# Seven products of halves for two pairs of down blocks in each half of the feed-forward layers

## The chip, the core and the metric

The kernel runs on one core of a Trainium2 chip. A core has a matrix engine (TensorE, PE in the profile, with its weight loads shown apart as PEld), a vector engine (VectorE, DVE), an activation engine (ScalarE, ACT), a general engine (GpSimd, POOL) and a queue engine (SyncE, SP). Each works through its own instructions strictly in the order of the program and waits on semaphores that other engines and transfers raise. The metric is device time in microseconds (us), the median of several runs.

## The reference

One decoder layer on 256 prompt tokens and 8 single-token samples, 264 tokens in all, model width 2048:

```python
def swiglu(x, wg, wu, wd):
    return (jax.nn.silu(x @ wg) * (x @ wu)) @ wd
...
h = h + 0.5 * swiglu(rmsnorm(h, norm_ffn1[l]), ffn1_gate[l], ffn1_up[l], ffn1_down[l])
mix, C_f, n_f, m_f, buf = mixing_block(rmsnorm(h, norm_mix[l]), w_in[l], ...)
h = h + mix
h = h + 0.5 * swiglu(rmsnorm(h, norm_ffn2[l]), ffn2_gate[l], ffn2_up[l], ffn2_down[l])
y = rmsnorm(h, norm_final)
```

The feed-forward width is 5504, or 43 blocks of 128. All inputs are float32. The change touches the down products (`@ wd`) of both feed-forward layers.

## The kernel before

Everything lies transposed: features on the 128 partitions, the 264 tokens in the free dimension. `h` is the running state in 16 blocks of 128 features; two neighbours share a tile (`hpair`). A float32 product is made of float16 parts: every operand is cut into a high part `hi` (ScalarE, `high`, L220) and a low part `lo` = rest (VectorE, `low`, L228), and each 128x128 weight block is three matmuls over 264 columns (`three`, L287 to L289): hi by x hi, hi by x lo, lo by x hi.

**Order of the program.** Layer 1, then the mixing block, then layer 2, then the final norm. A layer is worked in two halves of its 43 blocks: blocks 0 to 21, then 22 to 42. In each half first all gate and up products of its blocks (16 weight blocks each, "gate-up stage"), which leave the activations `a` of 22 or 21 blocks, then 16 down products over these ("down stage"), each added to one block of `h` (L846, VectorE). In the second half `done(db)` follows each of them: in layer 1 it cuts the block for the mixing block and squares it on GpSimd, in layer 2 it squares it and scales it with the final gain on ScalarE. The last two down products of layer 2 are made in two spans of tokens by `end`.

**Weights.** `plan` lists pieces of at most 8 weight blocks in the order of use. `fetch` issues a piece's transfer on SP, its hi on ScalarE and its lo on VectorE. `product` calls `fetch` after each piece that it consumes, so that five pieces (AHEAD) are under way or ready; hi, lo and raw have six buffers each. In a gate-up stage `lag` holds a piece's lo back until the next fetch, so that it stands behind the next piece's hi; in a down stage it was off. `tick` counts products (and halves of them); `at(delta, fn)` puts work into the program at a later tick, so the order on every engine is what this hand-made agenda gives.

**Seven products.** For 23 blocks (SEVEN) gate and up are not two plain products. Their 2 x 16 weight blocks are taken as a 2 x 2 matrix of halves, the tokens as two halves of 132, and seven products of halves (Strassen's scheme in Winograd's form) give the four quarters: 7 x 8 x 3 = 168 matmuls over 132 columns (L409) where two plain products have 2 x 16 x 3 = 96 over 264. `chunk_by_seven` issues them in two parts, c = 0 (72 matmuls, weights `sa`) and c = 1 (96 matmuls, weights `sb`), with one plain block between them. `by_seven` puts the quarters together on VectorE (tile `y7`, L759 to L763). The activations' sums of halves, `forms`, are made once by `form` (ScalarE and GpSimd, L659 to L665) and `form_split`.

**Preparing their weights.** `prepare` makes a list of steps for each such job, and `prepare_step` performs one step after each piece that `product` consumes, up to `step_end`: load raw weights through GpSimd's queue (`load`, L331, two buffers), hi and lo of the plain quarters (`blocks`, `blocks_low`, tile `sa`), the sums of quarters (`all_sums`, L355 to L357, tile `ssum`; hi and lo of them in `sb`). A job has eight steps, and in a gate-up stage one job is needed every three blocks, which have eight pieces. At the end of the first half `step_end` stops the steps, and four more are allowed at the start of its down stage.

Two checks run beside the work: `watch` sums a strip of each product (L537), and `judge_early` (L556 to L580) compares all sums so far with bounds; it stands at the start of the product of block 7 in layer 2's last down stage.

## Time and profile before

| | us |
|---|---|
| time, median of 3 runs | 1816.19 (1815.84 to 1818.47) |
| the profiled execution, its own time | 1816.65 |
| its span in the trace | 1814.9 |
| layer 1: down stage of the first half | 242.80 to 361.98 |
| layer 1: gate-up of the second half | 361.98 to 580.80 |
| layer 1: down stage of the second half | 580.80 to 694.29 |
| layer 2: the same three stages | 1348.68 to 1467.87, to 1686.69, to 1794.54 |

The stage borders are the starts of TensorE's first matmul of each stage in the timeline. TensorE is busy for 1797.8 us, VectorE for 1388.2, ScalarE for 953.1 and GpSimd for 237.2. The granted TensorE clock is 0.998 of full speed over the run. A matmul's busy time in the profile has a modelled end, so what one costs is read from the distance between two starts, not from its duration. Idle time behind a row stands in brackets with what ended it.

### The profile page before, as it was taken

How to read it: one execution, taken by the hardware profiler on the slowest of the kernel's cores; microseconds unless marked ns; L12 is line 12 of the kernel's file. 1: busy time of each engine (PE TensorE's matmuls, PEld its weight loads, DVE VectorE, ACT ScalarE, POOL GpSimd, SP SyncE). 2: the span in 40 equal slices, each digit the busy share in tenths (PEclk: the TensorE clock that was granted, in tenths of full speed). 3: DMA queues.
4: the chain of work that ended last, by engine and by line, in shares of the span. 5: the costliest groups of instructions: out<-in, count | busy, mean ns of one | idle time of the engine just before them, and what ended most of it. 6: DMA issues, size and time to landing. Idle time of an engine off the chain costs nothing. (4 is left out here: it accounts for less than half of the span.)

```text
span 1814.9 us, 42526 instructions
## 1 busy us (share of the span) xinstructions
PE 1797.8 (99%) x17918; PEld 1591.0 (88%) x17918; DVE 1388.2 (76%) x2141; ACT 953.1 (53%) x1329; POOL 237.2 (13%) x338
## 2 busy tenths in 40 slices
PE   9999999999999999999999999999999999999997
PEld 7889988899998888888888888899988889999886
DVE  7888975579997657788888766789986459998564
ACT  7664554445554444567566645655554335554442
POOL 0310000000100222222121022410000001010110
PEclk9999999999999999999999999999999999999999
DMA  8665666645654565888887655756567646564553
GB/s 301 243 222 168 219 208 230 203 153 189 215 192 153 185 193 189 302 284 276 280 283 238 222 180 185 254 191 220 191 193 249 199 148 215 191 207 153 191 186 101
DMA packets 118615, 381.34 MB, mean 210 GB/s; under 512 B 15084, under 2 KB 24908, under 8 KB 118416
## 3 DMA queue, kind: packets, MB, share of 16 engines
q1 hardware_dynamic: 95952, 302.29, 50.1%
q0 software_dynamic: 21504, 75.81, 12.2%
q8 instruction: 142, 2.33, 0.5%
q10 hardware_dynamic: 960, 0.45, 0.1%
q14 instruction: 57, 0.47, 0.1%
HBM read 366.72 MB, written 11.78 MB: 209 GB/s over the span
## 5 line engine op out<-in xcount | busy, mean ns | idle before, releaser
L228 DVE SCALAR_TENSOR_TENSOR wlo<-wraw,whi 128x1024 f16<-128x1024 f32 (+2 forms) x600 | 688.2, 1172 | 103.5 <-ACT whi L220 102.9
L220 ACT ACTIVATE whi<-wraw 128x1024 f16<-128x1024 f32 (+2 forms) x600 | 580.0, 1000 | 160.6 <-PE ps L288 140.7
L289 PE MATMUL ps<-x,wlo 128*128 128x264 f16 x1952 | 538.8, 276 | 1.1 <-DVE wlo L228 1.1
L287 PE MATMUL ps<-x,whi 128*128 128x264 f16 x1952 | 538.8, 276 | 0.2 <-ACT whi L220 0.2
L288 PE MATMUL ps<-x,whi 128*128 128x264 f16 x1952 | 538.8, 276 | 0.0
L289 PEld LDWEIGHTS <-wlo 128*128 128x128 f16 x4522 | 442.5, 98 | 67.4 <-DVE wlo L228 2.4
L288 PEld LDWEIGHTS <-whi 128*128 128x128 f16 x4522 | 442.4, 98 | 66.2
L287 PEld LDWEIGHTS <-whi 128*128 128x128 f16 x4522 | 442.7, 98 | 65.6 <-issue 0.6
L289 PE MATMUL ps<-a,wlo 128*128 128x264 f16 (+2 forms) x1418 | 382.7, 273 | 0.4 <-DVE wlo L228 0.4
L287 PE MATMUL ps<-a,whi 128*128 128x264 f16 (+2 forms) x1418 | 382.8, 273 | 0.0
L288 PE MATMUL ps<-a,whi 128*128 128x264 f16 (+2 forms) x1418 | 382.8, 273 | 0.0
L287 PE MATMUL ps<-xm,whi 128*128 128x264 f16 x896 | 247.3, 276 | 0.0
L289 PE MATMUL ps<-xm,wlo 128*128 128x264 f16 x896 | 247.3, 276 | 0.0
L288 PE MATMUL ps<-xm,whi 128*128 128x264 f16 x896 | 247.3, 276 | 0.0
L220 ACT ACTIVATE sb<-ssum 128x2048 f16<-128x2048 f32 x46 | 87.9, 1911 | 181.2 <-DVE ssum L357 181.2
L409 PEld LDWEIGHTS <-sb 128*128 128x128 f16 x2208 | 128.8, 98 | 0.7
L846 DVE SCALAR_TENSOR_TENSOR h<-ps,h 128x264 f32<-128x264 f32 x62 | 26.7, 431 | 126.7 <-PE ps L289 126.7
L228 DVE SCALAR_TENSOR_TENSOR sb<-ssum,sb 128x2048 f16<-128x2048 f32 x46 | 105.2, 2288 | 8.0 <-ACT sb L220 5.6
L409 PE MATMUL ps<-f,sb 128*128 128x132 f16 x1656 | 99.0, 221 | 0.0
L409 PEld LDWEIGHTS <-sa 128*128 128x128 f16 x1656 | 97.1, 98 | 0.7
L331 POOL DMA_DIRECT2D sraw<-in_w2gu x48 | 34.6, 723 | 420.7 <-issue 371.5
L228 DVE SCALAR_TENSOR_TENSOR sa<-sraw,sa 128x1536 f16<-128x1536 f32 x46 | 81.8, 1778 | 3.1
(255 smaller groups left out, 1601.7 us busy)
## 6 DMA issues: line engine op xcount, KB each, us to landing
wraw<-in_w2gu SPq DMA_DIRECT2D x124, 512.0 KB, 4.6
wraw<-in_w1gu SPq DMA_DIRECT2D x120, 512.0 KB, 4.8
wraw<-in_win SPq DMA_DIRECT2D x112, 512.0 KB, 5.7
wraw<-in_w1d SPq DMA_DIRECT2D x80, 448.0 KB, 4.0
wraw<-in_w2d SPq DMA_DIRECT2D x80, 448.0 KB, 4.1
sraw<-in_w2gu POOLq DMA_DIRECT2D x48, 512.0 KB, 4.9
sraw<-in_w1gu POOLq DMA_DIRECT2D x44, 512.0 KB, 5.3
wraw<-in_wout SPq DMA_DIRECT2D x32, 512.0 KB, 4.8
```

Source lines behind the costliest of these rows:

```text
L220: nc.scalar.activation(dst, src, AF.Copy, scale=scale)
L228: nc.vector.scalar_tensor_tensor(dst, src, scale, hi, op0=ALU.mult, op1=ALU.subtract)
L287: nc.tensor.matmul(ps, wh, xk[:, 0, :], start=first, stop=False)
L288: nc.tensor.matmul(ps, wh, xk[:, 1, :], start=False, stop=False)
L289: nc.tensor.matmul(ps, wl, xk[:, 0, :], start=False, stop=last)
L331: queue.dma_start(raw[:, 2 * g : 2 * g + 2], blocks[:, :, ks[c], :])
L409: nc.tensor.matmul(out, w[:, f, k, :], b(k)[:, part, :], start=(k + term == 0), stop=(k == 7 and term == 2),)
L846: nc.vector.scalar_tensor_tensor(h[db], ps, 0.5 / (sw * sa[layer]), h[db], op0=ALU.mult, op1=ALU.add)
```

## The change

Two pairs of down blocks in each half of each layer, blocks (6, 7) and (10, 11), now go by seven products over the first 16 of the half's activation blocks; the remaining 6 (first half) or 5 (second half) blocks of each are a short plain product ("rest"). A pair's parts alternate with plain blocks: part 0, block 8, rest 6, part 1, block 9, rest 7, and likewise for 10 and 11 with 12 and 13. The raw weights of these pairs come through GpSimd's queue, as jobs of the same list of steps. For the right-hand side `form` adds hi and lo of two activation blocks on GpSimd, makes their sums there, and `form_split` cuts them (ScalarE, VectorE): eight forms for each half, started with the up product of the half's last block. The steps pause from that block's start until down block 3, and afterwards no job is prepared before the one before it has been begun. The sums of weights are written over the raw weights instead of into `ssum`, and the loads into these buffers stand after the low part of the sums. In the down stages `lag` is on. Also: `Norm.cut` gives the low part of a block one tick later, `judge_early` stands at the last product before `end`, two kinds of checking tiles use `y7`'s buffer, and some tiles of the mixing block have buffers in other pools.

```diff
+SEVEN_DOWN = {"1": ((3, 5), (3, 5)), "2": ((3, 5), (3, 5))}
 PAIRS = sum(len(v) for v in SEVEN.values())
+PAIRS += sum(len(v) for halves in SEVEN_DOWN.values() for v in halves)
...
+def down_order(pairs, n):
+
+    order = []
+    for p in range(-(-n // 2)):
+        if p in pairs:
+            for c in range(2):
+                order += [("seven", p, c), ("one", 2 * p + 2 + c), ("rest", 2 * p + c)]
+        elif p - 1 not in pairs:
+            order += [("one", db) for db in range(2 * p, min(2 * p + 2, n))]
+    return order
...
+        jobs = []
+        for half, blocks_ in enumerate(HALVES):
+            jobs += [(j, gu[j, 0], gu[j, 1]) for j in SEVEN[layer] if j in blocks_]
+            cut = slice(blocks_[0], blocks_[0] + KB)
+            for p in SEVEN_DOWN[layer][half]:
+                jobs.append((("d", half, p), d[2 * p][:, cut], d[2 * p + 1][:, cut]))
...
-            sums[0] = s = pool.tile([128, 4, 4, 128], F32, tag="ssum", name="ssum")
-            nc.vector.tensor_tensor(s[:, 2], raw[:, 2], raw[:, 3], op=ALU.add)
-            nc.vector.tensor_tensor(s[:, 3], s[:, 2], raw[:, 1], op=ALU.subtract)
+            nc.vector.tensor_tensor(raw[:, 3], raw[:, 2], raw[:, 3], op=ALU.add)
+            nc.vector.tensor_tensor(raw[:, 1], raw[:, 3], raw[:, 1], op=ALU.subtract)
...
-                s = -4 if n == 0 else 8 * n + (-2, -1)[c]
+                s = -4 if n == 0 else 8 * n + (-2, 0)[c]
                 steps.setdefault(s, []).append((load, j, c))
...
         hi, lo = formed.pop((j, c))
+        step_end[0] += 8 * (c == 0)
...
+            def form(k):
+                b = form_blocks()
+                for n, i in enumerate((k + 8, k)):
+                    y = act[blocks[i]]
+                    side.tensor_tensor(
+                        b[:, 2 * n : 2 * n + 2].rearrange("p s t -> p (s t)"), y[:, 0, :],
+                        y[:, 1, :], op=ALU.add,
+                    )
+                forms.append(form_sums(b))
...
-                    if half_size and half == 0 and j == blocks[-1]:
-
-                        step_end[0] = step_no[0]
                     lag[0] = half_size and j >= (3 if start is not None else 1)
+                    if downs and j == blocks[-1]:
+
+
+                        paused, step_end[0] = step_end[0], min(step_end[0], step_no[0] + 1)
+                        for k in range(9):
+                            when = 2 + int(1.5 * k) / 2
+                            if k:
+                                at(when, form_split, k - 1)
+                            if k < 8:
+                                at(when, form, k)
...
-                if half == 0 and half_size:
-                    step_end[0] += 4
+                lag[0] = bool(downs)
...
+                def down_by_seven(p):
+                    y, halves = assemble(seven.pop(p))
+
+                    def summed():
+                        both = hpair[p].rearrange("p i t -> p (i t)")
+                        nc.vector.scalar_tensor_tensor(
+                            both, y[:, 0:4].rearrange("p s t -> p (s t)"), scale, both,
+                            op0=ALU.mult, op1=ALU.add,
+                        )
+
+                    at(1, halves)
+                    at(1, summed)
+
+                for kind, db, *c in down_order(downs, KB - apart):
+                    if kind == "seven":
+                        if c[0] == 0:
+                            seven[db] = [bank() for _ in range(3)]
+                        chunk_by_seven(("d", half, db), c[0], x, forms, seven[db])
+                        if c[0] == 1:
+                            down_by_seven(db)
+                        continue
+                    if downs and db == 3:
+                        step_end[0] = paused
+                    over = range(KB if kind == "rest" else 0, len(x))
+                    ps = product((layer, "d", half, db), x, over)
...
                 lag[0] = False
                 release()
-                for db in range(KB - apart):
...
-        at(2 * NFB + 2 * KB - 8, judge_early)
+
+        more = 2 * sum(len(p) for p in SEVEN_DOWN["2"])
+        at(2 * NFB + 2 * KB + more - 2, judge_early)
```

Three places show how instructions move. Names: `wlo` is the lo of a plain piece (896 is 7 weight blocks, 1024 is 8, 768 is 6), `sraw` the raw weights of a seven-job, `sb` the lo of its sums, `fa` the lo of a form, `h` an update of the state, `stat` a watched strip, `y` and `twins` the putting together.

VectorE, first half's down stage, near its end. Before, from the update of block 12 on, each product had an update, its strip and three lo parts:

```order
L846 SCALAR_TENSOR_TENSOR h_86<-ps,h_86 128x264
L537 TENSOR_REDUCE stat<-ps 128x1
L228 SCALAR_TENSOR_TENSOR wlo<-wraw,whi 128x896
L228 SCALAR_TENSOR_TENSOR wlo<-wraw,whi 128x1024
L228 SCALAR_TENSOR_TENSOR wlo<-wraw,whi 128x896
L846 SCALAR_TENSOR_TENSOR h_86<-ps,h_86 128x264
```

And now, from the state's update by the second pair (blocks 10 and 11) to the update of block 13:

```order
L919 SCALAR_TENSOR_TENSOR h_85<-y_5049,h_85 128x528
L248 SCALAR_TENSOR_TENSOR wlo<-wraw,whi 128x896
L381 TENSOR_TENSOR sraw<-sraw 128x512
L382 TENSOR_TENSOR sraw<-sraw 128x512
L383 TENSOR_TENSOR sraw<-sraw 128x2x512
L248 SCALAR_TENSOR_TENSOR wlo<-wraw,whi 128x896
L248 SCALAR_TENSOR_TENSOR sb_5085<-sraw,sb_5084 128x4x512
L248 SCALAR_TENSOR_TENSOR wlo<-wraw,whi 128x1024
L381 TENSOR_TENSOR sraw<-sraw 128x512
L382 TENSOR_TENSOR sraw<-sraw 128x512
L383 TENSOR_TENSOR sraw<-sraw 128x2x512
L939 SCALAR_TENSOR_TENSOR h_86<-ps,h_86 128x264
```

Behind these stand the strip, one more `wlo` of 896, the second `sb`, the update of block 11 with its strip, and the `wlo` of block 15's second piece. The sums of a job stand now inside the down stage, ahead of the lo parts that TensorE needs next.

VectorE, first half's down stage, between the updates of blocks 2 and 3. The first four rows are these, with the sums of the first job's other half and the second `sb` behind them:

```order
L939 SCALAR_TENSOR_TENSOR h_81<-ps,h_81 128x264
L564 TENSOR_REDUCE stat<-ps 128x1
L248 SCALAR_TENSOR_TENSOR fa_3952<-form_t,fa_3952 128x528
L248 SCALAR_TENSOR_TENSOR wlo<-wraw,whi 128x896
L381 TENSOR_TENSOR sraw<-sraw 128x512
L382 TENSOR_TENSOR sraw<-sraw 128x512
L383 TENSOR_TENSOR sraw<-sraw 128x2x512
L248 SCALAR_TENSOR_TENSOR wlo<-wraw,whi 128x1024
L248 SCALAR_TENSOR_TENSOR sb_4051<-sraw,sb_4050 128x4x512
```

Before, the four steps stood at the stage's start, ahead of and just behind the update of block 0; now forms and steps stand between the updates of blocks 0 to 5.

VectorE, the end of layer 2's last down stage, from the update of block 13 on (L603 to L595 are `judge_early`):

```order
L939 SCALAR_TENSOR_TENSOR h_86<-ps,h_86 128x264
L564 TENSOR_REDUCE stat<-ps 128x1
L603 TENSOR_SCALAR ok<-stat 128x260
...
L595 TENSOR_REDUCE verdict_26082<-okp 128x1
L248 SCALAR_TENSOR_TENSOR wlo<-wraw,whi 128x896
L939 SCALAR_TENSOR_TENSOR h_85<-ps,h_85 128x264
L564 TENSOR_REDUCE stat<-ps 128x1
L248 SCALAR_TENSOR_TENSOR wlo<-wraw,whi 128x896 x2
L1020 SCALAR_TENSOR_TENSOR h_87<-ps,h_87 128x136
```

Before, the judging stood behind the update of block 6, with nine products to follow; now only three lo parts, all of block 15, stand behind it.

129 lines of the change are left out of this document (81 added, 48 removed).

## The prediction

> **What bounds the kernel now.** I read the page's busy times first, then TensorE's timeline for the distance of starts, then the stages, then what makes TensorE's lo weights.
>
> ```profile
> span 1814.9 us, 42526 instructions
> PE 1797.8 (99%) x17918; PEld 1591.0 (88%) x17918; DVE 1388.2 (76%) x2141; ACT 953.1 (53%) x1329; POOL 237.2 (13%) x338
> ```
>
> TensorE is busy for all but 17 us, so work taken from it is time taken from the kernel, as long as its weights come early enough. The price of a matmul, by starts (gate-up stage, plain products, then part 0 of a pair):
>
> ```profile
> 116.74 0.28 PE L287 MATMUL ps<-x,whi 128*128 128x264 f16 x1
> ...
> 117.64 0.28 PE L289 MATMUL ps<-x,wlo 128*128 128x264 f16 x1
> 117.76 2.92 PE L409 MATMUL ps<-x,sa 128*128 128x132 f16 x48
> 120.52 1.54 PE L409 MATMUL ps<-f,sa 128*128 128x132 f16 x24
> 121.90 0.28 PE L287 MATMUL ps<-x,whi 128*128 128x264 f16 x1
> ```
>
> Eight steps of 264 columns take 117.64 - 116.74 = 0.90 us, 0.1125 each. The 72 of 132 columns take 121.90 - 117.76 = 4.14 us, 0.0575 each. The down stages, with TensorE, VectorE, ScalarE and GpSimd busy:
>
> ```profile
> 243.00:362.00 119.00, 118.79 (x1057) 103.08 (x1056) 69.54 (x90) 50.98 (x51) 2.88 (x4) 1.00 0.67 221
> 362.00:581.00 219.00, 219.00 (x2524) 199.29 (x2522) 188.15 (x255) 109.49 (x128) 14.42 (x20) 1.00 0.55 179
> 581.00:694.00 113.00, 113.00 (x1007) 98.28 (x1006) 66.92 (x99) 47.16 (x65) 21.93 (x29) 1.00 0.61 194
> ```
>
> In a down stage VectorE has 50 us of 119 free; in the gate-up stage, with a job every three blocks, it is busy for 188 of 219, and TensorE still never idles. The one wait of the down stages is at the start of the first half's, in both layers:
>
> ```profile
> 265.18 0.28 PE L288 MATMUL ps<-a,whi 128*128 128x264 f16 x1
> 265.67 0.29 PE L289 MATMUL ps<-a,wlo 128*128 128x264 f16 x1 [0.21 <-DVE wlo L228]
> 1371.56 0.29 PE L289 MATMUL ps<-a,wlo 128*128 128x264 f16 x1 [0.21 <-DVE wlo L228]
> ```
>
> By starts it is 265.67 - 265.18 - 0.11 = 0.38 us each. It is what four steps of one job's preparation cost there. So the lo parts are the second bound, and the question is whether two whole jobs and eight forms fit into each down stage.
>
> **The change part by part.** *TensorE.* A pair gives up 2 x 16 x 3 = 96 matmuls at 0.1125 = 10.80 us and takes 168 at 0.0575 = 9.66. That is -1.14 us, eight times: **-9.1 us**. The rest blocks cost what they cost before. That shorter matmuls hide their weight loads is seen in the 23 pairs of before. The Trainium skill speaks against it: "TensorE: Matmul & The Clock Gate", Back-to-back issue gap, gives about 81 ns a matmul of 128 columns in a stream of loads and matmuls; an estimate by it is 168 x 0.081 = 13.6 us a pair, eight times +2.8 or about +22 us. The trace has 57.5 ns for 132 columns in such a stream, so it does not agree.
>
> *VectorE, ScalarE.* Durations, from the groups of the first down stage by shape, and of the whole run:
>
> ```profile
> L228 DVE SCALAR_TENSOR_TENSOR wlo<-wraw,whi 128x896 f16<-128x896 f32 x29 | 31.5, 1085 | 8.7 <-ACT whi L220 8.7
> L846 DVE SCALAR_TENSOR_TENSOR h<-ps,h 128x264 f32<-128x264 f32 x15 | 6.5, 431 | 34.2 <-PE ps L289 34.2
> L228 DVE SCALAR_TENSOR_TENSOR sb<-ssum,sb 128x2048 f16<-128x2048 f32 x1 | 2.3, 2291 | 2.0 <-ACT sb L220 2.0
> L228 DVE SCALAR_TENSOR_TENSOR sa<-sraw,sa 128x1536 f16<-128x1536 f32 x1 | 1.8, 1750 | 0.0
> L228 DVE SCALAR_TENSOR_TENSOR f<-form_t,f 128x528 f16<-128x528 f32 x16 | 11.9, 742 | 0.0
> L220 ACT ACTIVATE sb<-ssum 128x2048 f16<-128x2048 f32 x46 | 87.9, 1911 | 181.2 <-DVE ssum L357 181.2
> ```
>
> and from the timeline, where neighbours overlap a little, by starts:
>
> ```profile
> 259.04 0.68 DVE L355 TENSOR_TENSOR ssum<-sraw 128x512 f32<-128x512 f32 x1
> ...
> 260.48 1.22 DVE L357 TENSOR_TENSOR ssum<-sraw,ssum 128x1024 f32<-128x1024 f32 x1
> ...
> 476.42 0.27 ACT L749 COPY m<-ps 128x132 f32<-128x132 f32 x1 [0.54 <-PE ps L409]
> 476.72 0.43 DVE L759 TENSOR_TENSOR y<-ps,m 128x264 f32<-128x264 f32 x1 [0.38 <-ACT m L749]
> 478.42 0.71 DVE L767 TENSOR_TENSOR y<-y,rstd 128x528 f32<-128x528 f32 x1
> ```
>
> Less 0.08 of overlap: sums 2.6, `sb` 2.2, `sa` 1.7, a lo piece 1.0 (7 blocks) or 1.14 (8), update with strip 0.42, putting a pair together 1.7, form 0.66. Adding a pair to the state (128x528, not in the trace) lies by the row of the same size at 0.66; bounds 0.4 (128x264) and 1.1. A pair's preparation is 2 x (2.6 + 2.2 + 1.7) = 13.0 us; with 8.0 of lo pieces (six of 7 and 8 blocks, two of 6), 1.7 of updates and 2.4 of putting together, VectorE has 25.1 us of work for a pair, its two rests and its two plain products. TensorE needs 9.66 + 2 x (66 + 18) x 0.1125 = 28.6 us for them. It fits on the average, 88% of the time, and the gate-up stage runs at 188.15 / 219 = 86% without a wait. What counts is where it bunches, in the first half:
>
> (a) From block 2's update to the last piece of block 5 the rows of the change (front part) add up to 0.42 + 0.66 + 1.0 + 2.6 + 1.14 + 0.8 (wait for ScalarE's 1.9 us on `sb`) + 2.2 + 1.0 + 2.6 + 0.42 + 0.66 + 1.0 + 2.2 + 0.66 + 1.14 = 18.5 us. TensorE asks for that piece after three products of 66 x 0.1125 = 7.43 less its own 2.7, 19.6 us, less 0.3 that the update begins late, plus 0.2 as lo comes third: 19.5. Spare 1.0, if nothing slows VectorE. GpSimd works on forms at that time:
>
> ```profile
> 98.39 1.75 DVE L228 SCALAR_TENSOR_TENSOR sa<-sraw,sa 128x1536 f16<-128x1536 f32 x1
> 101.54 2.30 DVE L228 SCALAR_TENSOR_TENSOR sa<-sraw,sa 128x1536 f16<-128x1536 f32 x1
> ...
> L663 POOL TENSOR_TENSOR form_t<-form_b x16: 733/746/1384, 50.7 to 1176.1; 128x264 f32<-128x264 f32 x16
> L664 POOL TENSOR_TENSOR form_t<-form_b,form_t x16: 462/465/1866, 51.6 to 1177.5; 128x132 f32<-128x132 f32 x16
> ```
>
> The same instruction took 0.55 us longer beside a form, and the form's own subtraction between 0.46 and 1.87. Two or three such delays bring 1.0 down to somewhat under nothing; I take 0.3 late. Bounds: 0, and 3 (three forms of some 4 us stand beside this stretch; 13 us of VectorE's work slowed by 0.55 / 1.75 = 31% is 4.0, less the spare 1.0). A form is three subtractions and two adds of fp16 parts that the trace lacks; by L663 0.75 each (0.46 to 1.87), 3 to 5 us a form, against one every three quarters of a product, 5.6 us: GpSimd keeps up.
>
> (b) From the end of the second pair to the second piece of block 15, VectorE needs 1.7 + 0.66 + 1.0 + 2.6 + 1.0 + 0.95 + 2.2 + 1.14 + 2.6 + 0.42 + 1.0 + 0.5 + 2.2 + 0.42 + 1.0 = 19.4 us (0.95 and 0.5 are waits for ScalarE), and begins 0.7 late behind the copy. TensorE reaches that lo after block 13, rest 11 (18 x 0.1125), block 14 and a piece, 7.43 + 2.03 + 7.43 + 2.36 + 0.2 = 19.5. So **0.6 to 0.8 late**; bounds 0 and 2. No pair follows to give time back.
>
> Both together 1.1 us, in two layers **+2.2**, bounds 0 and 10. The second half enters its down stage with the first job's `sa` and first sums done, and no third job follows: only (a) is there, with some 3 us spare. GpSimd has squares there too, each behind its update, with the forms and two loads queued behind them, and ScalarE's hi pieces stand behind the cut of each form. Eight forms of 4.2 us, four squares of some 1.4 with their additions (a square alone is 0.62, by the end's row below) and two loads of 1.4 make 42 us from 3.5 before the stage's start, so the last form is there at about 39; part 0 wants it after 6 x 63 x 0.1125 + 48 x 0.0575 = 45.3. Nothing, bounds 0 and 3 for each. The old wait goes: **-0.8**.
>
> *The loads.* In-place sums keep a raw buffer until `sb` is made:
>
> ```profile
> 462.99 1.44 POOL L331 DMA_DIRECT2D sraw<-in_w1gu  x2 [6.61 <-issue]
> 466.22 2.28 DVE L228 SCALAR_TENSOR_TENSOR sb<-ssum,sb 128x2048 f16<-128x2048 f32 x1
> 473.67 1.47 ACT L220 ACTIVATE sa<-sraw 128x1536 f16<-128x1536 f32 x1
> sraw<-in_w1gu POOLq DMA_DIRECT2D x44, 512.0 KB, 5.3
> ACT whi L220 <- PE ps L288: 140.7, 93, 5.8
> ```
>
> The load goes out at 468.5 instead of 463.0, is issued by 469.9 and lands 5.3 us later, 475.2: ScalarE's `sa` waits 1.5 us. Behind it stand the hi pieces, but ScalarE itself waits for TensorE to free buffers (140.7 us in all), it runs five pieces of 2.7 us ahead. Nothing; without that cover 1.5 us for each of 19 jobs.
>
> *The end.* The judging stands now behind block 13:
>
> ```profile
> 1737.05 0.74 DVE L575 TENSOR_SCALAR ok<-stat 128x254 f32<-128x254 f32 x1
> ...
> 1741.08 3.08 DVE L228 SCALAR_TENSOR_TENSOR wlo<-wraw,whi 128x896 f16<-128x896 f32 x3
> ...
> 1785.91 0.22 PE L287 MATMUL ps<-a,whi 128*128 128x136 f16 x1
> ...
> 1786.62 0.62 POOL L678 TENSOR_TENSOR sq<-h 128x264 f32<-128x264 f32 x1 [5.64 <-DVE stat L537]
> ...
> 1787.70 1.77 ACT L220 ACTIVATE whi<-wraw 128x896 f16<-128x896 f32 x2
> ...
> 1788.34 0.22 PE L289 MATMUL ps<-a,wlo 128*128 128x136 f16 x1
> ```
>
> It takes 4.0 us. Count from the end of rest 11: block 13 ended 1.7 before, its update and strip end at -1.0, the judging at 3.0, block 15's first lo at 4.0. TensorE wants it after 63 matmuls of (1788.34 - 1785.91) / 41 = 0.059 us, at 3.8: 0.2 late. The update of block 11 waits behind the judging too, and for it GpSimd's square, ScalarE's gain and the last hi; the last lo is then at 7.7 for 6.4. **+1.3**, bounds 0.2 and 2.5.
>
> *The rest*: a low part one tick later, tiles in other pools, `y7` for checks: nothing; VectorE has 46 us free in the second half's down stage, and if a lo of the last block were late it would cost its 0.4 us.
>
> Sum: -9.1 + 2.2 - 0.8 + 1.3 = -6.4 us. The profiled execution took 1816.65, so 1810.2; the median is 0.46 below it: **1809.8 us**.
>
> **The rivals.** *All fits*: VectorE's rows are no slower than alone and (a), (b) vanish; the end alone costs. 1816.2 - 9.1 - 0.8 + 1.3 = 1807.6. For it: the gate-up stage with 86% of VectorE's time has no idle matmul. Against: the 0.38 at 265 us.
>
> *VectorE and GpSimd slow each other*: (a) costs its bound of 3 in both layers and the second halves, with 3 spare against 4.0, 1 each. 2 x (3 + 0.8) + 2 x 1 = 9.6 in place of 2.2 gives 1817.2, at half of it 1813.5: within what is no change. For it: 1.75 against 2.30. Against: beside 2.6 us of forms VectorE lost 0.55, the rest of the waiting was GpSimd's own.
>
> *The lock, slower*: each GpSimd instruction shuts VectorE out for its whole time. Three forms of 3.1 us fall into (a), 9.3 us, of which 1.0 is spare: 8.3 late, twice; in the second halves the same forms and squares against about 3 spare, 6.3, twice. 1809.8 + 2 x 8.3 + 2 x 6.3 = 1839; it decides from 3 us for each stage on, where the gain is used up. The Trainium skill has this as its rule: by "SBUF — State Buffer", SBUF: two separate sides, the two engines' shared port is an exclusive lock for a whole instruction, and the loser blocks. The trace agrees in that both slow down, not in the size on VectorE's side. Against it, then: 0.55 us lost, not 2.6.
>
> *Weights bound the short matmuls*, at the time of one load:
>
> ```profile
> L409 PEld LDWEIGHTS <-sa 128*128 128x128 f16 x1656 | 97.1, 98 | 0.7
> ```
>
> 168 x 0.098 = 16.5 us a pair, +5.7, 1862; 23 pairs at 57.5 ns, loads beside matmuls, say no.
>
> **How the numbers follow.** The forecast (1807.9 to 1812.5) 0.53; all fits 0.24; slowing each other 0.17, 1812.6 to 1817; the lock 0.05; weights 0.01. The range runs from 1806.3 (no loss anywhere) to 1814.5, and leaves out the upper part of the third and the last two. 0.2% is 3.6 us, about what can be told from no change: faster below 1812.6, 0.77; same 0.17; slower above 1819.8, 0.06.
>
> **What would show it.** Part 0 of a down pair takes 4.14 us and part 1 5.52. The first half's down stage lasts 119.2 - 0.4 - 2.3 + 1.1 = 117.6, the second half's of layer 1 113.5 - 2.3 = 111.2. Idle matmuls `<-DVE wlo` stand at block 5 and at block 15, under 1.5 us each, and at the two spans of the end. If block 5 waits over 2 us, the slowing is right; `sa` and `wlo` rows beside forms then grow by a third or more. Wrong altogether: waits on `sa`, `sb` or `fa` themselves, or on `whi` behind late raw weights in the gate-up stage.

## The result, and the profile after

The changed kernel takes 1875.21 us (median of 5 runs, 1872.13 to 1878.89) against 1817.47 for the kernel before beside it: 1.0320 times as long, 95% interval 1.0308 to 1.0332. The forecast was 1809.8 with a range from 1806.3 to 1814.5. The profiled execution took 1872.13 us.

The page after, and the waits of TensorE over the whole run (columns: engine, tile and line <- what released it: us in total, times, the longest):

```profile
span 1870.4 us, 43935 instructions
PE 1805.7 (97%) x18494; PEld 1596.8 (85%) x18494; DVE 1526.7 (82%) x2269; ACT 991.2 (53%) x1369; POOL 438.2 (23%) x530
...
PE ps L309 <- DVE wlo L248: 34.3, 23, 3.3
PE ps L436 <- DVE sb L248: 7.4, 4, 2.7
PE ps L307 <- ACT a L240: 4.2, 2, 2.7
```

VectorE is busy for 138.5 us more, GpSimd for 201, and TensorE, which in the four down stages had waited only twice, 0.38 us each time, now waits in all of them. Stage by stage, from the first matmul of one to the first of the next (the last: to the end of the span), in us:

| stage | before | after | difference |
|---|---|---|---|
| layer 1, gate-up of the first half (from 0) | 242.8 | 244.5 | +1.7 |
| layer 1, down, first half | 119.2 | 132.2 | +13.0 |
| layer 1, gate-up, second half | 218.8 | 218.8 | 0 |
| layer 1, down, second half | 113.5 | 123.2 | +9.7 |
| mixing block | 422.0 | 422.1 | 0 |
| layer 2, gate-up, first half | 232.3 | 241.0 | +8.7 |
| layer 2, down, first half | 119.2 | 129.7 | +10.5 |
| layer 2, gate-up, second half | 218.8 | 218.8 | 0 |
| layer 2, down, second half, and the end | 128.2 | 140.1 | +11.8 |

So the four down stages, forecast at 1 to 2 us shorter each, are 10 to 13 us longer, and one gate-up stage that the forecast left alone is 8.7 us longer. The saved matmuls are there: part 0 of a pair takes 306.40 - 302.26 = 4.14 us, part 1 takes 321.37 - 315.85 = 5.52, as forecast (timeline of TensorE, first down stage):

```profile
302.26 2.92 PE L436 MATMUL ps<-a,sa 128*128 128x132 f16 x48
305.02 1.54 PE L436 MATMUL ps<-fa,sa 128*128 128x132 f16 x24
306.40 0.28 PE L307 MATMUL ps<-a,whi 128*128 128x264 f16 x1
...
315.85 1.54 PE L436 MATMUL ps<-a,sb 128*128 128x132 f16 x24
317.23 4.30 PE L436 MATMUL ps<-fa,sb 128*128 128x132 f16 x72
321.37 0.28 PE L307 MATMUL ps<-a,whi 128*128 128x264 f16 x1
```

Adding up over the whole trace by how much each distance between two starts exceeds 0.1125 us (264 columns) or 0.0575 (132), waits over 0.3 us make 59.4 us, 5.2 before, and matmuls at half rate behind such waits 11.8, 1.2 before. The growth of these two less the 9.1 us of the pairs, 54.2 + 10.6 - 9.1 = 55.7, accounts for the 55.5 by which the span grew. Three things made the waits, and one more made them dearer.

**ScalarE behind GpSimd.** ScalarE's timeline at the start of layer 1's first down stage, and TensorE's:

```profile
246.88 0.93 ACT L240 ACTIVATE whi<-wraw 128x896 f16<-128x896 f32 x1
252.61 0.64 ACT L240 ACTIVATE fa<-form_t 128x528 f16<-128x528 f32 x1 [4.80 <-POOL form_t L663]
253.16 0.93 ACT L240 ACTIVATE whi<-wraw 128x896 f16<-128x896 f32 x1
254.00 0.41 ACT L240 ACTIVATE a<-tc 128x264 f16<-128x264 f32 x1
...
251.47 0.28 PE L309 MATMUL ps<-a,wlo 128*128 128x264 f16 x1
254.46 0.38 PE L307 MATMUL ps<-a,whi 128*128 128x264 f16 x1 [2.71 <-ACT a L240]
```

The cut of the first form stands on ScalarE ahead of the high part of the last activation, and waits 4.80 us for GpSimd; TensorE needs that activation, and waits for it. Behind the later cuts it is the hi parts of the weights that stand and wait, and VectorE's lo parts behind these. Over the run ScalarE waits 60.0 us for forms.

**VectorE beside GpSimd.** VectorE's lo parts, sums and GpSimd's form between blocks 3 and 5 of that stage:

```profile
278.34 1.35 DVE L248 SCALAR_TENSOR_TENSOR wlo<-wraw,whi 128x896 f16<-128x896 f32 x1
279.62 1.17 DVE L381 TENSOR_TENSOR sraw<-sraw 128x512 f32<-128x512 f32 x1
280.82 1.06 DVE L382 TENSOR_TENSOR sraw<-sraw 128x512 f32<-128x512 f32 x1
281.91 1.65 DVE L383 TENSOR_TENSOR sraw<-sraw 128x1024 f32<-128x1024 f32 x1
...
278.82 2.51 POOL L831 TENSOR_TENSOR form_b<-a 128x264 f32<-128x264 f16 x2
281.41 1.07 POOL L661 TENSOR_TENSOR form_t<-form_b 128x264 f32<-128x264 f32 x1
282.56 1.33 POOL L662 TENSOR_TENSOR form_t<-form_b,form_t 128x132 f32<-128x132 f32 x1
```

Sums that took 0.68, and 1.22 for the last, take 1.17, 1.06 and 1.65. GpSimd's subtraction of 132 columns, 0.46 alone, takes 1.33 here and up to 2.39.

The ends of these rows show how: they alternate. VectorE's first sum ends at 280.79, GpSimd's additions at 281.33, VectorE's second sum at 281.88, GpSimd's first subtraction at 282.48, VectorE's last sum at 283.56 and GpSimd's next subtraction 0.33 later. Over this trace, such a subtraction of 132 columns that began while VectorE worked on two inputs other than a product (`ps`) ended 0.32 to 0.33 us after that instruction in all 62 cases, though it took anything from 0.53 to 2.39 us; and a lo part of 896 columns that began while GpSimd worked ended 0.95 us after GpSimd's instruction in all 49. So the two take turns, one whole instruction at a time, and each waits out what is left of the other's. VectorE's updates, which read a product, keep their 0.42.

**A late load in the gate-up stages.** The page has for ScalarE's high parts of the plain quarters

```profile
L240 ACT ACTIVATE sa<-sraw 128x1536 f16<-128x1536 f32 x62 | 91.3, 1473 | 44.7 <-DMA sraw<-in_w2gu 22.3
```

44.7 us of waiting for raw weights; before, this row had no wait at all. In layer 2's first gate-up stage:

```profile
1306.69 1.48 ACT L240 ACTIVATE sa<-sraw 128x1536 f16<-128x1536 f32 x1 [5.19 <-DMA sraw<-in_w2gu]
1308.08 0.41 ACT L240 ACTIVATE a<-tc 128x264 f16<-128x264 f32 x1
1308.39 0.25 ACT L791 COPY m<-ps 128x132 f32<-128x132 f32 x1
```

Behind it stand an activation's high part and the copy with which a pair of products is put together; VectorE waits for both, then has everything at once, and TensorE waits for `sb` three times and for `sa` once there.

**The clock.** After a long wait TensorE runs at half rate (timeline after):

```profile
291.15 0.28 PE L308 MATMUL ps<-a,whi 128*128 128x264 f16 x1
294.74 0.29 PE L309 MATMUL ps<-a,wlo 128*128 128x264 f16 x1 [3.31 <-DVE wlo L248]
...
295.76 0.43 PE L307 MATMUL ps<-a,whi 128*128 128x264 f16 x1
...
298.40 0.43 PE L307 MATMUL ps<-a,whi 128*128 128x264 f16 x1
298.62 0.32 PE L308 MATMUL ps<-a,whi 128*128 128x264 f16 x1
```

It is 0.22 us from start to start instead of 0.1125, for some 3 us. The granted clock of a stretch, the third figure from the end, is 0.50 there:

```profile
295.40:298.40 3.00, 3.00 (x15) 2.04 (x14) 3.00 (x3) 2.34 (x3) 2.92 (x2) 0.50 0.53 153
```

Of the nine waits over 2.1 us eight are followed by 0.9 to 1.7 us lost in this way; of the 33 from 0.3 to 1.9 us none costs more than 0.12 so, but for the one right behind the long wait that ends at 254.46.

### The profile page after: what moved, and what is told of

Its sections match the earlier page's. It is cut to its first block, busy times and chain, and to the rows that moved or that the text cites. A ratio compares the mean times of both kernels' runs of the same rounds, so it can differ in the third digit from the quotient of the medians.

```text
span 1870.4 us, 43935 instructions
## 1 busy us (share of the span) xinstructions
PE 1805.7 (97%) x18494; PEld 1596.8 (85%) x18494; DVE 1526.7 (82%) x2269; ACT 991.2 (53%) x1369; POOL 438.2 (23%) x530
## 3 DMA queue, kind: packets, MB, share of 16 engines
q8 instruction: 146, 2.39, 0.5%
## 5 line engine op out<-in xcount | busy, mean ns | idle before, releaser
L248 DVE SCALAR_TENSOR_TENSOR wlo<-wraw,whi 128x1024 f16<-128x1024 f32 (+4 forms) x568 | 678.2, 1215 | 78.8 <-ACT whi L240 78.0
L240 ACT ACTIVATE whi<-wraw 128x1024 f16<-128x1024 f32 (+4 forms) x568 | 549.2, 996 | 73.7 <-PE ps L308 38.8
L308 PEld LDWEIGHTS <-whi 128*128 128x128 f16 x4266 | 418.9, 98 | 68.4 <-issue 4.5
L307 PEld LDWEIGHTS <-whi 128*128 128x128 f16 x4266 | 419.1, 98 | 65.4 <-ACT whi L240 2.9
L309 PE MATMUL ps<-a,wlo 128*128 128x264 f16 (+2 forms) x1162 | 317.2, 276 | 33.2 <-DVE wlo L248 33.2
L307 PE MATMUL ps<-a,whi 128*128 128x264 f16 (+2 forms) x1162 | 317.4, 276 | 5.5 <-ACT a L240 4.2
L308 PE MATMUL ps<-a,whi 128*128 128x264 f16 (+2 forms) x1162 | 317.3, 276 | 1.3 <-DVE a L248 1.3
L240 ACT ACTIVATE sb<-sraw 128x2048 f16<-128x2048 f32 x62 | 118.5, 1911 | 219.0 <-DVE sraw L383 219.0
L436 PEld LDWEIGHTS <-sb 128*128 128x128 f16 x2976 | 175.2, 98 | 9.0 <-DVE sb L248 8.1
L248 DVE SCALAR_TENSOR_TENSOR sb<-sraw,sb 128x2048 f16<-128x2048 f32 x62 | 145.0, 2338 | 34.5 <-ACT sb L240 33.7
L436 PEld LDWEIGHTS <-sa 128*128 128x128 f16 x2232 | 130.9, 98 | 2.5 <-DVE sa L248 1.5
L240 ACT ACTIVATE sa<-sraw 128x1536 f16<-128x1536 f32 x62 | 91.3, 1473 | 44.7 <-DMA sraw<-in_w2gu 22.3
```

Of the source, the lines that this page charges most:

```text
L240: nc.scalar.activation(dst, src, AF.Copy, scale=scale)
L248: nc.vector.scalar_tensor_tensor(dst, src, scale, hi, op0=ALU.mult, op1=ALU.subtract)
L307: nc.tensor.matmul(ps, wh, xk[:, 0, :], start=first, stop=False)
L308: nc.tensor.matmul(ps, wh, xk[:, 1, :], start=False, stop=False)
L309: nc.tensor.matmul(ps, wl, xk[:, 0, :], start=False, stop=last)
L436: nc.tensor.matmul(out, w[:, f, k, :], b(k)[:, part, :], start=(k + term == 0), stop=(k == 7 and term == 2),)
```

## The experiments

Where a kernel makes no forms, or cuts something else in their place, the pairs' results are not what they should be; their matmuls are the same in number and size. Each median below is followed by its ratio to runs of the kernel before taken beside it (medians 1816.1 to 1817.2) and that ratio's 95% interval.

### Are the side edits enough? No pairs

```diff
-SEVEN_DOWN = {"1": ((3, 5), (3, 5)), "2": ((3, 5), (3, 5))}
+SEVEN_DOWN = {"1": ((), ()), "2": ((), ())}
```

> The changed kernel with no down pair at all (the four lists empty), all the other edits kept: sums of weights over the raw weights, the second load of a job one fetch later, the low part of a block one tick later, the judging at the last product. No job, form or short matmul is left in the down stages, and they are again sixteen plain products. Theory 'late load' (the waits for sa and sb in layer 2's first gate-up stage, 8.7 us there and 1.7 in layer 1, come from the in-place sums and the loads behind them): that stage stays at about 241 us against 232.3 before, the end keeps some 2.5 us, and the time is about 1816 + 8.7 + 1.7 + 2.5 = 1829. Rival 'pairs' (the waits there need the pairs' jobs or forms): 1817 to 1819, that stage at 232.3.

1847.57 us, ratio 1.0165 (1.0148 to 1.0182). Layer 2's first gate-up stage is 239.2 us, its waits are nearly those of the changed kernel, 5.3 us for `sb` and 1.0 for `sa` against 5.0 and 1.3; so the loss there needs no pair. But 18 us more than expected were lost elsewhere: both first-half down stages are 10 us longer than before.

```profile
PE ps L307 <- ACT a L240: 11.5, 2, 5.7
PE ps L436 <- DVE sb L248: 8.0, 3, 2.7
```

Without a pair nothing stops the steps at the last block (the stop of before was replaced by one that depends on the pairs), and ScalarE's cut of the sums then stands ahead of the last activation's high part and waits 5.74 us for VectorE's sums. That is a wait of this run's own; the changed kernel doesn't have it.

### What do the forms cost? None, free cuts, cuts alone

No forms (`e2`), the matmuls read parts of the activations:

```diff
-                            if k:
-                                at(when, form_split, k - 1)
-                            if k < 8:
-                                at(when, form, k)
+                            if k:
+                                forms.append(None)
...
+            if forms[0] is None:
+                return lambda k: x[k + 8 * (n // 2)][:, :, (left, right)[n % 2]]
             return lambda k: forms[k][:, :, n]
```

Free cuts (`e3`): GpSimd makes every form, and the cuts read two blocks of the state:

```diff
-                forms[k] = form_parts(apool, f"fa{k}", forms[k])
+                still = hpair[7].rearrange("p i t -> p (i t)").rearrange("p (s t) -> p s t", s=4)
+                forms[k] = form_parts(apool, f"fa{k}", still)
```

Cuts alone (`e4`): the same, and GpSimd makes no form.

```diff
-                b = form_blocks()
-                for n, i in enumerate((k + 8, k)):
...
-                forms.append(form_sums(b))
+                forms.append(None)
```

> The changed kernel without the forms: nothing is added on GpSimd or cut on ScalarE and VectorE, and the pairs' short matmuls read parts of the activations in the forms' place (same number and size of matmuls, so the output of the pairs is not what it should be). Theory 'forms' (GpSimd's instructions slow VectorE, or ScalarE's hi parts stand behind cuts that wait for GpSimd): most of the 52 us of waits and slow clock in the four down stages vanish, 1875 - 40 to 52 = 1823 to 1835. Theory 'burst' (too much preparation stands between blocks 3 and 6 once the steps go on, whatever GpSimd does): the waits for lo parts at blocks 4 and 5 stay, only the wait for the last activation (about 4.5 us in layer 1, 2 in layer 2) goes, 1860 to 1868.

> The changed kernel with all of the forms' work on GpSimd, but the cuts of the forms (ScalarE, VectorE) read two blocks of the state that are long ready, in the place of GpSimd's result: no cut waits for GpSimd, so nothing on ScalarE waits behind one; the pairs' output is not what it should be. Theory 'order' (hi parts behind cuts that wait): the wait for the last activation and a good part of the lo waits go, about 1875 - 30 = 1845, and VectorE's instructions stay as long as they are beside GpSimd. Theory 'slowing' (GpSimd and VectorE slow each other): the lo waits of blocks 4 and 5 stay, 1862 to 1870.

> As the run before, and the forms' work on GpSimd is left out: only the cuts on ScalarE and VectorE remain, of the same size, from the ready state (the pairs' output is not what it should be). The difference to the run before is what GpSimd's instructions cost by being there. 'Slowing': 15 to 30 us faster than that run, about 1830 to 1840, with the lo part of 896 columns back at 1.08 us and the sums at 0.69, 0.69, 1.22. 'Order': the same as that run within 4 us. 'Burst': both stay above 1855.

No forms: 1824.72 (1.0046, 1.0032 to 1.0061). Free cuts: 1852.50 (1.0191, 1.0174 to 1.0208). Cuts alone: 1824.80 (1.0046, 1.0030 to 1.0063). So the forms cost 50 us of the 58, and the cuts' own time on ScalarE and VectorE costs nothing that shows. Of the 50, 27.7 go with GpSimd's instructions though nothing waits for their results (free cuts less cuts alone), and the other 23 are there when cuts wait for them (1.032 less 1.0191). Both theories hold, each with about half.

What GpSimd's presence does is seen in VectorE's groups by shape in layer 1's first down stage, and in the stretch after block 3 (busy us of PE, PEld, DVE, ACT, POOL). Free cuts:

```profile
L248 DVE SCALAR_TENSOR_TENSOR wlo<-wraw,whi 128x896 f16<-128x896 f32 x23 | 29.6, 1292 | 0.0
L248 DVE SCALAR_TENSOR_TENSOR wlo<-wraw,whi 128x1024 f16<-128x1024 f32 x15 | 20.8, 1397 | 1.9 <-ACT whi L240 1.9
...
246.00:369.00 123.00, 118.18 (x1199) 104.06 (x1197) 108.24 (x127) 59.64 (x64) 59.80 (x52) 0.99 0.61 198
268.00:294.00 26.00, 22.29 (x189) 18.55 (x188) 25.51 (x25) 13.30 (x14) 24.82 (x20) 0.96 0.42 123
```

Cuts alone:

```profile
L248 DVE SCALAR_TENSOR_TENSOR wlo<-wraw,whi 128x896 f16<-128x896 f32 x23 | 24.7, 1082 | 0.0
L248 DVE SCALAR_TENSOR_TENSOR wlo<-wraw,whi 128x1024 f16<-128x1024 f32 x16 | 19.2, 1216 | 3.7 <-ACT whi L240 3.7
...
245.00:363.00 118.00, 116.27 (x1198) 103.28 (x1197) 96.50 (x128) 59.53 (x64) 8.65 (x12) 1.00 0.62 207
268.00:294.00 26.00, 26.00 (x269) 23.15 (x267) 24.40 (x29) 13.45 (x15) 2.88 (x4) 1.00 0.68 230
```

Lo parts last 1.29 and 1.40 us instead of 1.08 and 1.22, VectorE is busy for 11.7 us more in the stage (108.24 for 96.50). In the stretch of 26 us it has 24.4 us of work without GpSimd and TensorE never waits; beside GpSimd it works through 25 instructions instead of 29 in the same time, without a pause, and TensorE waits. The Trainium skill, "Perfetto Trace Analysis", Optimizing Scalar/DVE Operations, says that the two engines share a read port, so that moving work between them might not help. The run with forms on VectorE, below, agrees: it gains only 7 us of 58.

In layer 2's second half free cuts recover nothing (140.8 us, cuts alone 128.5). There ScalarE also scales each block behind GpSimd's square of it, and the squares stand behind forms: in the run with free cuts the scaling waited up to 9.0 us, with hi parts behind it:

```profile
1745.68 0.52 ACT L992 ACTIVATE h<-h,vecs 128x264 f32<-128x264 f32 x1 [9.01 <-POOL sq L720]
1746.10 0.93 ACT L240 ACTIVATE whi<-wraw 128x896 f16<-128x896 f32 x1
```

That this queue is the cause is not shown: in the run with no form on GpSimd, below, the stage takes 141.2 us all the same. By stage, the two profiled executions differ by 4.9, 5.6, 6.2 and 12.3 us in the four down stages; how the 27.7 us divide between VectorE's waits for its turn and such queues was not measured apart.

### The load

```diff
-                (2, blocks, 0), (3, blocks_low, 0), (3, blocks, 1), (4, blocks_low, 1),
+                (2, blocks, 0), (3, blocks_low, 0), (4, blocks, 1), (5, blocks_low, 1),
```

> The changed kernel with one edit: the parts of a job's second plain quarters (ScalarE's hi and VectorE's lo of sa, second half) one step later, so that the load that now goes out later has 2.7 us more. Theory 'late load': ScalarE's wait for the raw weights (up to 5.2 us, with the activation's hi and the pair's putting together queued behind it) goes or halves, the waits for sb in layer 2's first gate-up stage too: 1875 - 5 to 9 = 1866 to 1870, that stage at 233 to 236 us. Rival 'VectorE is full there': that stage stays at 239 to 242, the time within 2 us of 1875.

1865.98 us, 1.0278 (1.0261 to 1.0295): 7.6 us less than the changed kernel's ratio. Layer 2's first gate-up stage is back at 232.3 us, to the tenth what it was before, with no wait of TensorE in it. So the late load is the cause there. The down stages, at 129.0, 124.9, 129.3 and 142.4, are between 3 us shorter and 2 us longer than in the changed kernel.

### Forms at another place

Forms in the gate-up stage, in place in one tile (`e5`; `e7` with the edit above; `e8` with `db == 1` for the step's restart besides):

```diff
-                        for k in range(9):
-                            when = 2 + int(1.5 * k) / 2
-                            if k:
-                                at(when, form_split, k - 1)
-                            if k < 8:
-                                at(when, form, k)
+                    if downs and i == len(blocks) - 10:
+                        for k in range(8):
+                            at(1.5 + 2.5 * k, form, k)
+                            at(3 + 2.5 * k, form_split, k)
```

In these three one of a form's four sums is taken from another pair of quarters, of the same size, so their output is not what it should be, unlike what the expectation says; the work is of the same size.

> The changed kernel with the forms made during the gate-up stages, as soon as the activations are there (one every 2.5 products from ten blocks before the stage's end, each cut one and a half products after its sums), in place in one tile; output complete. The down stages then hold no form at all. If forms in the down stages are what costs there (the runs without them: 47 to 50 us), the down stages go back to about 122, 111, 122, 128 us, as without forms, and the time is 1875 - 48 = 1827 plus what eight forms cost a gate-up stage. Theory 'room': GpSimd is free there (14 of 219 us busy), VectorE has 14% left and loses some 2 us a form: nothing to 4 us for the four stages, 1825 to 1832. Rival 'no room': VectorE at 86% has no lead to give, each form costs its 2 us: 1875 - 48 + 64 = 1890 at the most, 1840 to 1860 if a quarter to half of them show.

> Both edits: forms in the gate-up stages, second plain quarters one step later; output complete. If the two causes are apart, their gains add: 1827 - 8 = 1819 (1815 to 1824). Left would be the end (2.5 us), block 15 (3 us) and small waits, against the 9 us that TensorE saves.

> As the run before, and the preparing goes on from down block 1 instead of block 3. Theory 'burst': sums and updates stand less close, the waits for lo parts in the first blocks go if there are any: 0 to 3 us faster than that run. Rival: without forms there is no burst to spread, the same within 1 us; or slower by 1 to 3, if the earlier steps fall on lo parts while the lead is short.

1860.86 (1.0245, 1.0228 to 1.0262), 1860.54 (1.0241, 1.0224 to 1.0258) and 1866.38 (1.0277, 1.0260 to 1.0294). The first-half down stages are indeed back at 119.0 and 117.6 us, but the second-half gate-up stages, which hid everything until then, are 225.9 and 224.9 instead of 218.8: 0.8 to 0.9 us for each form. The second-half down stages stay at 116.6 and 136.2, 5 and 8 us more than without forms (111.2 and 128.5), though they hold none; TensorE waits mostly for lo parts in their first 15 us, and the cause is open. VectorE's groups in the last part of a gate-up stage:

```profile
L248 DVE SCALAR_TENSOR_TENSOR wlo<-wraw,whi 128x1024 f16<-128x1024 f32 x25 | 34.5, 1391 | 0.0
L248 DVE SCALAR_TENSOR_TENSOR sa<-sraw,sa 128x1536 f16<-128x1536 f32 x8 | 16.6, 2071 | 0.0
```

Lo parts take 1.39 us for 1.22, and those of `sa` 2.07 for 1.75: the waits for a turn go along with the forms. "No room" was right. The two repairs didn't add, against what was expected: with both, the first gate-up stage of layer 2 gains 5.8 us and later stages lose nearly as much. Spreading the steps earlier cost 5.8 us, more than the 1 to 3 that its rival allowed, most of it in layer 1's first down stage (122.8 against 119.1); that it takes from the lead with which the stage starts is a guess.

### Forms on VectorE

```diff
-                    side.tensor_tensor(
+                    nc.vector.tensor_tensor(
...
-                forms.append(form_sums(b))
+                forms.append(form_sums(b, nc.vector))
...
-                            if k:
-                                at(when, form_split, k - 1)
                             if k < 8:
                                 at(when, form, k)
+                                at(when + 0.5, form_split, k)
```

> The changed kernel with the forms' five instructions on VectorE instead of GpSimd (a form's cut half a product after it, since VectorE would else wait for itself); output complete. By rows of VectorE of the same sizes (0.42 for 264 columns, 0.28 for 132) a form costs it 3 x 0.42 + 2 x 0.28 = 1.8 us, eight 14.6 us a stage, to the 107 of the run with cuts alone: 121 of some 122. In the run with GpSimd's forms and free cuts VectorE's own instructions took 118.9 us in that stage, 11.5 more than without GpSimd's. Theory 'slowing' (GpSimd's forms take nearly as much of VectorE's time as VectorE would need for them itself, and bring the waits of cuts, squares and loads besides): faster than the changed kernel, 1824.8 + 4 times 2 to 6 = 1833 to 1850. Rival 'VectorE has no room for them': 1865 or more. In layer 2's second half the squares wait for no form then: that stage at about 130 to 134 against 140.

1868.34 us, 1.0282 (1.0265 to 1.0299): the rival. The instructions have their lone durations again, and the stretch after block 3 is just as full:

```profile
L248 DVE SCALAR_TENSOR_TENSOR wlo<-wraw,whi 128x896 f16<-128x896 f32 x23 | 24.7, 1082 | 0.0
L831 DVE TENSOR_TENSOR form_b<-a 128x264 f32<-128x264 f16 x16 | 6.1, 425 | 0.0
L661 DVE TENSOR_TENSOR form_t<-form_b 128x264 f32<-128x264 f32 x8 | 3.5, 433 | 0.3
L662 DVE TENSOR_TENSOR form_t<-form_b,form_t 128x132 f32<-128x132 f32 x8 | 2.4, 296 | 0.3
L663 DVE TENSOR_TENSOR form_t<-form_t,form_b 128x132 f32<-128x132 f32 x8 | 2.4, 295 | 0.3
...
244.50:374.00 129.50, 121.39 (x1214) 105.66 (x1213) 113.25 (x170) 60.76 (x66) 8.65 (x12) 0.97 0.59 194
269.00:294.00 25.00, 22.04 (x196) 18.94 (x195) 24.45 (x42) 11.11 (x12) 1.44 (x2) 1.00 0.60 194
```

The forms take 6.1 + 3.5 + 2.4 + 2.4 = 14.4 us of VectorE's time in the stage when it makes them itself, and 11.7 when GpSimd makes them. (The 113.25 - 96.50 = 16.8 by which VectorE's busy time differs from cuts alone also holds one more `sa` of 1.75 us, which falls into the longer stage.) So the difference between the two kernels is only 7 us of 58. Cuts still wait on ScalarE in this run, 24.8 us for VectorE's forms where they waited 60.0 for GpSimd's, so it doesn't tell VectorE's time and waiting cuts apart. That layer 2's second half would be 130 to 134 us without squares behind forms was wrong: it is 141.2.

### The forecast's own kernel, and the end

Cuts alone with the load repaired (`e9`), and with the judging ten products before the last (`e11`; the last pair's sums get a fixed value first and aren't judged):

```diff
-        at(2 * NFB + 2 * KB + more - 2, judge_early)
+        at(2 * NFB + 2 * KB + more - 10, judge_early)
```

> The run with cuts alone (no form work on GpSimd, the cuts read the ready state, so the pairs' output is not what it should be), and the second plain quarters one step later. If GpSimd's forms and the late load are all that went wrong, this is what the forecast described, but for block 15 (1.9 us measured where 0.7 was expected) and the end (2.7 for 1.3): 1824.8 - 8.5 (layer 2's first gate-up stage) - 2 (layer 1's) = 1814. Rival 'a third cause in the side edits': above 1818.

> As the run before, with the judging ten products ahead of the layer's last instead of two (the sums of the last pair are set to a fixed value first, so that pair is not judged there). If the end's waits (0.95 + 0.74 + 1.00 us) are the judging's: 2.7 us faster than that run, about 1811.5, with no wait left at the two spans. Rival: the last lo parts are late for another reason, the same within 1 us.

1818.91 (1.0010, 1.0001 to 1.0020) and 1815.68 (0.9995, 0.9985 to 1.0004). The judging costs 3.2 us; one wait of 1.0 stays. The first is 5 us above what was expected and, at 1818.91, just in the range of its rival, a third cause. The cause lies in the repair, not in the changed kernel: with the later plain quarters the waits at blocks 14 and 15 in the first halves are 3.1 and 3.8 us instead of 1.9 and 1.1. With no form work, no late load and no judging at the end the kernel is level with the one before: 3.8 and 3.3 us of waits in the two first-half down stages and 1.3 in the last stage in that second run use up nearly all of the 9.1 us that the short matmuls save.

### Half of the pairs

```diff
+SEVEN_DOWN = {"1": ((5,), (5,)), "2": ((5,), (4,))}
...
+                            when = 2 + int(downs[0] * k / 2) / 2
...
+        at(2 * NFB + 2 * KB + more - 3, judge_early)
```

> A complete kernel with one pair in each half, late in the stage (blocks 10 and 11; in layer 2's second half 8 and 9), its eight forms spread over all the products before it (one in 1.25, or in 1, instead of one in 0.75), the second plain quarters one step later, and the judging a product earlier. TensorE saves 4 x 1.14 = 4.6 us. VectorE has 13 us less to prepare in each stage than with two pairs. Theory 'GpSimd's forms cost by falling where VectorE has no time to lose': with the forms spread and one pair, the down stages keep their lead: 1812 to 1818. Rival 'the forms cost wherever they stand' (in the changed kernel 50 us for 32 forms): 1820 to 1835, slower than before even with half of the pairs, since one pair needs all eight forms.

1836.37 us, 1.0103 (1.0086 to 1.0120). The rival again, 1 us above its range: gate-up stages are as before (237.7 and 232.3), each down stage is 3 to 6 us longer than before, though in layer 1's second half VectorE has a fifth of its time free. There TensorE waits 3.46 us at once for a lo part that stands on VectorE behind the low part of a job's sums; on ScalarE a hi part had stood behind the cut of the same sums, and that had waited 7.78 us for VectorE:

```profile
618.52 1.91 ACT L240 ACTIVATE sb<-sraw 128x2048 f16<-128x2048 f32 x1 [7.78 <-DVE sraw L383]
620.34 0.93 ACT L240 ACTIVATE whi<-wraw 128x896 f16<-128x896 f32 x1
...
625.78 0.40 PE L309 MATMUL ps<-a,wlo 128*128 128x264 f16 x1 [3.46 <-DVE wlo L248]
```

No run with pairs was clearly faster than the kernel before.

## Where the prediction was right, and where it failed

- **TensorE's saving** was right: 4.14 and 5.52 us for the parts. Layer 1's second half without GpSimd's forms takes 111.2 us, the forecast figure. The rival on weights was wrong: nothing waited for weight loads of short matmuls.
- **Step (a) failed** by the choice between its bounds: 0.3 us late of 0 to 3. Its sum, 18.5 us from block 2's update to the last lo piece of block 5, is what cuts alone take to the tenth (267.31 to 285.8, and no wait). With GpSimd's forms the same work takes 22.9 us with free cuts (268.96 to 291.9) and 22.3 in the changed kernel (277.30 to 299.6), so VectorE lost about 4 us there. That is three forms at 11.7 / 8 = 1.5 us each; the upper bound reached its 4.0, before the spare of 1.0, by another way, 31% on 13 us, and was near by luck. In the changed kernel the stretch also began late: block 2's update came 32.8 us into the stage, 22.5 with cuts alone, since TensorE had lost 4.7 us by then and VectorE had waited 1.03 and 3.23 us for ScalarE's cut and hi part. The forecast had counted 0.3 for a late update. With free cuts TensorE then waited 1.21 + 2.83 us at these blocks and lost 1.5 at half rate; in the changed kernel 1.18 + 1.16 + 3.47 + 1.05 and 1.6, 8.5 in all. The two or three single delays of 0.55 that were taken instead ignored that GpSimd works nearly without a pause through the whole stretch (24.82 of 26 us with free cuts).
- **"ScalarE's hi pieces stand behind the cut of each form. Nothing, bounds 0 and 3"** failed, and this is the larger omission. It was argued from when the last form must be ready (39 us for 45), not from what each cut holds up. Waiting cuts cost 23 us over the run, and the last activation alone 2.87 + 0.57 us and 1.2 at half rate in layer 1.
- **The loads at nothing** failed. The forecast gave ScalarE's `sa` 1.5 us of waiting and covered it by ScalarE's lead of five pieces. In the first-half gate-up stages ScalarE waited up to 5.2 us for them, and the cover was for hi parts, while the activation's high part behind it has none. It cost 8.7 us in layer 2's first gate-up stage, gone with the repair, and 1.7 in layer 1's, of which the repair gave back 1.1. Such waits were named as the sign of "wrong altogether".
- **Step (b)** was right in place and too small: TensorE waited 0.57 + 1.90 us at block 15 in layer 1 and 1.22 in layer 2 for 0.6 to 0.8 expected, with 2 as the bound; with cuts alone 1.9 and 1.1.
- **The end** had its three waits where the step put them: 0.96 + 0.74 + 1.00 = 2.7 for 1.3, a bit over the bound of 2.5. The judging took 4.6 us, from 1838.23 to 1842.84, for the 4.0 counted.
- **"The second half: nothing"** failed by 12 us in layer 1 and 13 in layer 2. With free cuts layer 1's loses 5.6 us instead of 12 against cuts alone, so cuts and GpSimd's instructions have about half each there; layer 2's stays as long with free cuts, and its cause is open.
- **The clock** had no term: 10.6 us at half rate behind long waits. The Trainium skill has it: "TensorE: Matmul & The Clock Gate", What's actually happening, gives half the clock after an idle window of some 3.4 us, and as long to recover. The trace agrees in the rate and in the 3 us, and shows that a wait of 2.2 us can be enough.
- The rival "VectorE and GpSimd slow each other" had the right engines and a ninth of the price (1817.2 less 1809.8, where 65.4 us were missing), since it counted VectorE's longer instructions only.

**The rival "the lock"** had the mechanism, and was put aside by a misread row. These are GpSimd's instructions beside the `sa` of 101.54 us in the kernel before:

```profile
101.46 0.77 POOL L663 TENSOR_TENSOR form_t<-form_b 128x264 f32<-128x264 f32 x1 [5.49 <-ACT form_b L659]
102.30 1.87 POOL L664 TENSOR_TENSOR form_t<-form_b,form_t 128x132 f32<-128x132 f32 x1
```

GpSimd's first ends at 102.22, `sa` 1.61 later at 103.84, GpSimd's second 0.33 after that. "0.55 us lost, not 2.6" is one turn waited for, not the price of a form: in the changed kernel a form has five instructions, hence up to five turns. The rival's size was off: VectorE pays only what is left of GpSimd's instruction, 1.5 us a form where the rival counted 3.1. That its 29.2 us stand near the measured 27.7 is partly luck, since it had 8.3, 6.3, 8.3 and 6.3 for the stages that show 4.9, 5.6, 6.2 and 12.3.

## What to carry to other kernels

Where an engine works strictly in order, an instruction that waits for a slower engine costs what stands behind it: for each cut that is put into a queue, name the next three instructions behind it and when these are wanted, before counting whether the total work fits. VectorE's 94% in 26 us ran without a wait of TensorE, but left no room for the 4 us that three forms beside it cost; work given to an engine that takes turns with the first one is only partly taken off it (here 11.7 of 14.4 us came back as longer instructions). And a kernel bound by one engine with a short lead loses twice for a long wait, by the wait and by the half clock behind it: here waits of up to 1.9 us cost only themselves, and one of 3 us cost 0.9 to 1.7 more.

## What was not expected of the hardware

- The half clock: 0.22 us for a 264-column matmul, for about 3 us, behind eight of the nine waits of 2.2 us or more, up to 1.7 us lost each time, and next to nothing behind waits of up to 1.9 us.
- VectorE and GpSimd take turns by whole instructions where both work on two inputs other than a product: GpSimd's subtraction ended 0.32 to 0.33 us after VectorE's instruction in all 62 cases. So the short ones suffer most: that subtraction, 132 columns, went from 0.46 to as much as 2.39 us behind VectorE's lo part of 2048 columns, while VectorE's lo part of 896 columns went from 1.08 to at most 1.64.
- GpSimd's addition of a block's fp16 hi and lo parts takes 0.68 us alone and up to 1.66 beside VectorE in the changed kernel.
